# Projecting the values of all heads at once, tokens on the partitions, with attention as one chain over the head pairs

## The chip, the cores and the metric

The kernel runs on one core of one Trainium2 chip. The metric is the device time of one execution in microseconds. Five engines each work through their own list of instructions: TensorE (PE, matrix products; PEld is its weight load), VectorE (DVE), ScalarE (ACT), GpSimd (POOL) and SyncE (SP). The order of each list is fixed when the kernel is built; semaphores hold an instruction until what it needs is there. SBUF is the on-chip memory with 128 partitions, PSUM the eight banks of 128 x 2 KB into which PE writes.

## The reference

One layer of a bidirectional encoder on 512 tokens with 2048 features, in float32. One input projection feeds two mixers that see the same normalised input: a Conformer convolution (1024 channels) and a two-dimensional neighbourhood attention (16 heads of 64) on a grid of 8 rows by 64 columns. The mixers' outputs are normalised each for itself and share one output projection; a gated feed-forward network follows.

```
xn   = rms_norm(x, attn_norm_g)
u_val, u_gate, q, k, v = split(xn @ w_in, [1024, 2048, 3072, 4096])
h      = depthwise_conv31(u_val * sigmoid(u_gate)) + bias
y_conv = silu(layer_norm(h))
y_na   = attention(q, k, v):  a token (r, c) sees all 8 rows and the 16 columns
         clip(c - 8, 0, 48) ... + 15;  softmax(q.k / 8 + rpb[head, dr, dc]) . v
x = x + concat(rms_norm(y_conv, conv_out_g), rms_norm(y_na, na_out_g)) @ w_out
gate, val = split(depthwise_conv3(rms_norm(x, ffn_norm_g) @ w_up))
x = x + (silu(gate) * val) @ w_down
out = rms_norm(x, final_norm_g)
```

## The kernel before

**Products.** Activations lie transposed: 16 tiles of 128 features x 512 tokens. Each float32 operand is split into a high and a low part in the format fp32r, and a product is three matmuls: high by high, high by low, low by high (`mm3`, L121 to L126). In the projections the weights are stationary and the activations move, so the result of `project` comes out with features on the partitions and tokens along the row.

**Weight units.** A unit is 512 KB of weights (128 x 1024): one transfer by SP into a buffer `raw` (ring of NR = 7), a copy to fp32r by ACT (`whi`, L113) and the remainder by DVE (`wlo`, L114), each into a ring of NW = 4. A unit feeds 24 matmuls of 128x512, eight blocks of features by three. `plan` lists the units in the order of use and `weights()` asks for each one AHEAD = 3 units early. One output block of `project` takes two units.

**Order.** `ORDER` says in which sequence output blocks are projected: `a` is one conv projection (gate and value, four units), `q` one pair of heads (q, k and v, six units). After every unit `tick` lets one step of each of two chains of generators run: `steps` (the first norm's statistics, then attention) and `asteps` (`group_a`: layer norm of the conv channels, from the pair NORM_AT on). After the tick, `late` runs `gated` for a finished conv projection: gate by the norm's scale, sigmoid on ACT, again the scale, the product `ch` (L316 to L320), and a conv of 31 taps on DVE: a start (L327, tensor_scalar) and 30 accumulating steps (L331) into `y`. These steps carry a later priority (`shifted(600)`), and the pairs of `y` tiles come out of the same ring `raw` as the weights.

**Who decides.** A scheduler at build time takes these calls with their priorities, its own estimate of times and the free buffers of each ring, and writes each engine's list. `pin` keeps marked instructions in the order of the program.

**Attention, a pair of heads at a time.** A pair is 128 features, and a block of 16 grid columns with all 8 rows (128 queries) sees a window of 32 columns (256 keys). DVE scales q and k by the norm (L383 into block order, L387 plain) and gathers four windows of v (`vw`, L392). `attend` loads four bias tables, turns v on PE (eight transposes `trv`, L411, and two copies `vt` on ACT, L413), and then runs in steps: scores (L425, 16 matmuls in four banks), softmax (DVE L432 scale and add the table, L434 maximum; ACT L437 exponentials with sums; DVE L438 reciprocal; ACT L440 scaling), two turns of the probabilities (`trp`, L450, with copies `pt`, L455), values (L464, 32 matmuls into the bank "po"), a copy `ao` (L484) and the sum of squares (L166, L167).

**Banks.** "mm" three banks for projections; "sc" two banks shared by scores and by the statistics `st`; "tr" two banks for turns and half of the scores; "po" one bank.

**After the projections.** `out_half(ma)` multiplies the conv half of `w_out` (16 units); its results wait in PSUM for the scale `ra` of the conv group's norm (L535). Then `norm_b`, `out_half(mb)` for attention's half, and the feed-forward network, which take three quarters of the time.

## Time and profile before

| | |
|---|---|
| median of three runs | 2055.87 us (2055.01 to 2056.87) |
| the profiled execution | 2055.28 us |
| its span on the core | 2053.5 us |
| mean granted TensorE clock | 0.997 of full |
| PE busy | 2034.3 us, 99% |
| DVE busy | 1663.1 us, 81% |
| ACT busy | 1061.4 us, 52% |
| first matmul of `out_half(ma)` | at 495.2 us |
| its last | at 597.1 us |

The span runs from the first to the last recorded instruction; the device time has 1.8 us more around it. A row of the timeline gives the start, the duration, the engine, the line and operation, and result<-operands; matmuls overlap in the pipeline, so their pace is the distance of their starts, not their duration. A row of a group gives the count, after the bar the busy time in all and the mean of one in ns, and after the second bar how long the engine was idle before them and what it waited for.

### The profile page before, as it was taken

The page shows a single profiled execution, that of the slowest core. Times are in us where ns is not written, and L with a number is a line of the kernel's source. Part 1 is how long each engine was busy: PE and PEld are TensorE (multiplying, and loading weights), DVE is VectorE, ACT ScalarE, POOL GpSimd, SP SyncE. Part 2 cuts the span into 40 slices and gives each one's busy share as a digit, 9 for nine tenths or more (in the row PEclk, how much of TensorE's full clock was granted, in tenths as well). Part 3 has the DMA queues.
Part 4 walks back from the last instruction along what each step waited for, and adds up shares of the span by engine and source line. Part 5 has one row for each costly group of instructions (what it writes and reads, how often), then busy time and mean ns, then how long its engine had stood idle before and what let it go on. Part 6 is the DMA issues. An engine that isn't in the chain of part 4 may idle for free.

```text
span 2053.5 us, 28580 instructions
## 1 busy us (share of the span) xinstructions
PE 2034.3 (99%) x10816; PEld 1736.5 (85%) x10816; DVE 1663.1 (81%) x2319; ACT 1061.4 (52%) x1726; POOL 156.3 (8%) x186
## 2 busy tenths in 40 slices
PE   9999999999999999999999999999999999999997
PEld 7888888887788998888888888888888888888887
DVE  7996697686577898888888878888788888889876
ACT  6244424457445555555555555555554554555562
POOL 0000000000001001111111111111111111110110
PEclk9999999999999999999999999999999999999998
DMA  7332333236237435555465565555555565554672
GB/s 253 109 107 83 100 97 111 84 103 237 82 113 182 127 116 139 127 148 142 120 151 147 124 144 144 130 137 144 135 133 143 126 147 143 133 139 124 148 211 83
DMA packets 97209, 275.38 MB, mean 134 GB/s; under 512 B 10928, under 2 KB 11696, under 8 KB 97072
## 3 DMA queue, kind: packets, MB, share of 16 engines
q1 hardware_dynamic: 71712, 227.40, 34.9%
q0 software_dynamic: 25216, 46.15, 14.8%
q8 instruction: 85, 1.39, 0.3%
q14 instruction: 52, 0.43, 0.1%
q10 hardware_dynamic: 144, 0.01, 0.0%
HBM read 218.99 MB, written 54.53 MB: 133 GB/s over the span
## 4 chain that ended last, share of the span: by engine, by line
PE 94%; DVE 3%; issue 1%; ACT 1%; DMA 1%; SPq 0%; DVEq 0%; ACTq 0%
PE pu L660 23%; PE pu L665 12%; PE pd L126 8%; PE pd L124 8%; PE pd L125 8%; PE pj L124 7%; PE pj L126 7%; PE pj L125 7%; PE po L124 3%; PE po L126 3%; PE po L125 3%; PE pu L124 1%; PE pu L126 1%; PE pu L125 1%; PE sc L425 1%
## 5 line engine op out<-in xcount | busy, mean ns | idle before, releaser
L114 DVE TENSOR_TENSOR wlo<-raw,whi 128x1024 fp32r<-128x1024 f32 x364 | 444.5, 1222 | 246.0 <-ACT whi L113 223.6
L113 ACT ACTIVATE whi<-raw 128x1024 fp32r<-128x1024 f32 x364 | 384.3, 1058 | 489.0 <-PE pj L125 186.2
L660 PE MATMUL pu<-xc,whi 128*128 128x512 f32 x2240 | 573.5, 392 | 0.2 <-ACT pl L672 0.2
L660 PEld LDWEIGHTS pu<-xc,whi 128*128 128x128 f32 x2240 | 408.6, 189 | 74.0 <-ACT pl L672 0.5
L665 PEld LDWEIGHTS pu<-xc,wlo 128*128 128x128 f32 x2240 | 305.6, 190 | 21.9
L665 PE MATMUL pu<-xc,wlo 128*128 128x256 f32 x2240 | 312.3, 282 | 0.0
L124 PE MATMUL pj<-xh,whi 128*128 128x512 f32 x640 | 251.7, 397 | 0.0
L126 PE MATMUL pd<-hh,wlo 128*128 128x512 f32 x640 | 249.1, 391 | 2.2 <-DVE wlo L114 2.2
L126 PE MATMUL pj<-xh,wlo 128*128 128x512 f32 x640 | 250.0, 391 | 0.0
L124 PE MATMUL pd<-hh,whi 128*128 128x512 f32 x640 | 250.0, 391 | 0.0
L125 PE MATMUL pj<-xl,whi 128*128 128x512 f32 x640 | 249.8, 390 | 0.1
L125 PE MATMUL pd<-hl,whi 128*128 128x512 f32 x640 | 249.1, 389 | 0.0
L779 POOL DMA_DIRECT2D x2d<-pdc x160 | 139.3, 872 | 1167.7 <-ACT pdc L778 1064.9
L672 ACT ACTIVATE pl<-pu 128x256 f32<-128x256 f32 x280 | 105.2, 380 | 173.3 <-PE pu L660 173.3
L331 DVE SCALAR_TENSOR_TENSOR y<-ch,prm,y 128x500 f32<-128x500 f32 (+14 forms) x240 | 173.8, 742 | 4.5
L113 ACT ACTIVATE whi<-ws 128x1024 fp32r<-128x1024 f32 x132 | 139.8, 1059 | 67.9 <-PE pu L660 43.5
L114 DVE TENSOR_TENSOR wlo<-ws,whi 128x1024 fp32r<-128x1024 f32 x132 | 161.2, 1221 | 1.3 <-ACT whi L113 1.2
L126 PEld LDWEIGHTS pd<-hh,wlo 128*128 128x128 f32 x640 | 120.2, 188 | 30.9 <-DVE wlo L114 5.7
L124 PEld LDWEIGHTS pj<-xh,whi 128*128 128x128 f32 x640 | 120.1, 188 | 28.7 <-issue 3.9
L778 ACT ACTIVATE pdc<-pd 128x512 f32<-128x512 f32 x160 | 93.9, 588 | 95.9 <-PE pd L126 95.8
L126 PEld LDWEIGHTS pj<-xh,wlo 128*128 128x128 f32 x640 | 120.1, 188 | 26.2 <-DVE wlo L230 0.8
L125 PEld LDWEIGHTS pj<-xl,whi 128*128 128x128 f32 x640 | 120.2, 188 | 25.7 <-issue 1.1
(178 smaller groups left out, 2767.9 us busy)
## 6 DMA issues: line engine op xcount, KB each, us to landing
raw<-in_w_up SPq DMA_DIRECT2D x176, 512.0 KB, 3.6
raw<-in_w_down SPq DMA_DIRECT2D x88, 512.0 KB, 3.6
x2d<-pdc POOLq DMA_DIRECT2D x160, 256.0 KB, 4.6
raw<-in_w_in SPq DMA_DIRECT2D x76, 512.0 KB, 3.7
raw<-in_w_out SPq DMA_DIRECT2D x32, 512.0 KB, 3.8
x<-in_xT SPq DMA_DIRECT2D x32, 256.0 KB, 5.3
tab<-in_tab SPq DMA_DIRECT2D x32, 256.0 KB, 5.1
x2d<-x SPq DMA_DIRECT2D x16, 256.0 KB, 2.2
```

Source lines behind the costliest of these rows:

```text
L113: i = nc.scalar.activation(hi[:, :n], raw[:, :n], AF.Copy)
L114: j = nc.vector.tensor_sub(lo[:, :n], raw[:, :n], hi[:, :n].bitcast(F32))
L124: nc.tensor.matmul(ps, hi[:, a], mh, start=start, stop=False)
L125: nc.tensor.matmul(ps, hi[:, a], ml, start=False, stop=False)
L126: return nc.tensor.matmul(ps, lo[:, a], mh, start=False, stop=stop)
L331: nc.vector.scalar_tensor_tensor(y[:, a:b], h[:, a + j - PAD:b + j - PAD], prm[:, o + j:o + j + 1], y[:, a:b], op0=ALU.mult, op1=ALU.add)
L425: m = nc.tensor.matmul(banks[b // 2 * 2 + j][:, b % 2, :], q[hp, b * P:(b + 1) * P], grid(k, KC0[b], KW)[hp], start=True, stop=True)
L660: return nc.tensor.matmul(ps, w[0][:, k * P:(k + 1) * P], comb[c][k], start=k == 0, stop=k == U - 1)
L665: nc.tensor.matmul(ps[:, H:], w[1][:, k * P:(k + 1) * P], comb[c][k][:, :H], start=False, stop=False)
L672: nc.scalar.activation(to, ps, AF.Copy)
L778: nc.scalar.activation(t, ps, AF.Copy)
L779: nc.gpsimd.dma_start(xd[d], t, accum_op=ALU.add)
```

## The change

1. The values of all 16 heads are projected in one go (`project_v`, step `v` of the order). The activations are stationary (128 tokens of `xh` or `xl` at a time), the weights move (512 of the 1024 value features at a time), so v comes out with tokens on the partitions and needs no turning. There are two halves of features, each into four banks: the first into the three "mm" banks and "po", the second into the two "tr" and the two "sc" banks. A unit of the new input `w_v` holds two blocks of features by 512 columns, and feeds 24 matmuls of 128x512 as before; there are 16 units. ACT copies the results out with the norm's scale per token (`rtok`): eight tiles `vg` and six tiles `vx`, which hold the windows that straddle two 128-token slices.
2. The projection input is regrouped on the host: `xG` holds the tokens in groups of eight grid columns with all rows. q is then written plain, k with a permutation, `ch` and `ao` are written back in the plain token order, and the bias tables are laid out to match. The residual still reads `xT`.
3. Attention is one chain over all pairs in place of a generator for each: for pair p the tables; then the values of pair p-1, the scores and the softmax of p in one tick; a tick of nothing; the turn of the second half of the blocks; the turn of the first. The softmax works in place in the table's tile. There are no `trv`, `vt` and `vw`.
4. The order of projections is `aaaav aq aq aq aq qqqq` (written without gaps), with four units for a `q`, and `group_a` starts at pair 4 in place of 5.

The counts: matmuls 128x512 of the projections stay 1920 (1536 `pj` and 384 `pv`); 64 transposes go from PE, 32 products from DVE; on ACT 16 copies and 4 table loads go and 20 copies come. SP issues 500 transfers in both.

```
-ORDER = "aaqaqaqaaqaqaqqq"
-NORM_AT = 5
+ORDER = "aaaav" + "aq" * 4 + "qqqq"
+NORM_AT = 4
+NG = GW // 8
...
+        if by_token is not None:
+            by_token.append(y)
...
-        last = pin(nc.sync.dma_start(x1[k], xT[k]))
+        last = pin(nc.sync.dma_start(x1[k], xG[k]))
...
+        if step == "v":
+            for half in range(2):
+                for u in range(KD // 2):
+                    plan.append(lambda half=half, u=u: unit(w_v[half, u], U * P))
+            continue
         i = next(a_ if step == "a" else q_)
-        for n in ((NC_ + i, i) if step == "a" else (2 * NC_ + j * NP_ + i for j in range(3))):
+        for n in ((NC_ + i, i) if step == "a" else (2 * NC_ + j * NP_ + i for j in range(2))):
...
+    vg, vx = [], []
+
+    def project_v():
+
+        for half in range(2):
+            if half:
+                sc = psa.tile([P, 2, S], F32, tag="sc", name="pv")
+                banks = [psa.tile([P, S], F32, tag="tr", name="pv", bufs=2) for _ in range(2)] + [sc[:, 0], sc[:, 1]]
+            else:
+                banks = [psm.tile([P, S], F32, tag="mm", name="pv") for _ in range(3)]
+                banks.append(psa.tile([P, S], F32, tag="po", name="pv"))
+            for u in range(KD // 2):
+                wh, wl = weights()[:2]
+                for k in range(2):
+                    kk, f = 2 * u + k, slice(k * S, (k + 1) * S)
+                    for t, ps in enumerate(banks):
+                        xh, xl = (x[:, t * P:(t + 1) * P] for x in xs[kk])
+                        nc.tensor.matmul(ps, xh, wh[:, f], start=kk == 0, stop=False)
+                        nc.tensor.matmul(ps, xl, wh[:, f], start=False, stop=False)
+                        m = nc.tensor.matmul(ps, xh, wl[:, f], start=False, stop=kk == KD - 1)
+                tick(m)
+                while late and rstd:
+                    late.pop(0)()
+            y = rtok[0]
+            vg.append([t2("vg") for _ in banks])
+            vx.append([t2("vx") for _ in banks[1:]])
+            for t, ps in enumerate(banks):
+                nc.scalar.activation(vg[half][t], ps, AF.Copy, scale=y[:, t:t + 1])
+                for x, rows in ((t - 1, slice(0, DH)), (t, slice(DH, P))):
+                    if 0 <= x < len(vx[half]):
+                        nc.scalar.activation(vx[half][x][rows], ps[rows], AF.Copy, scale=y[rows, t:t + 1])
...
-        nc.vector.tensor_mul(h, pv, g)
+        by = "p (g r c) -> p r g c"
+        nc.vector.tensor_mul(h.rearrange("p (r g c) -> p r g c", r=WH, g=NG), pv.rearrange(by, r=WH, g=NG),
+                             g.rearrange(by, r=WH, g=NG))
...
+    def attention():
+
+        before = None
+        for p in range(NP_):
+            while len(qk) <= p:
+                yield
+            ts = tables(p)
+            yield
+            if before:
+                values(*before)
+            banks = scores(p, not before)
+            softmax(banks, ts)
+            yield
+            yield
+            pts = {}
+            pts[2], pts[3] = turn(ts, 2)
+            yield
+            pts[0], pts[1] = turn(ts, 0)
+            before = p, pts
+        yield
+        values(*before)
+        yield
...
+        if step == "v":
+            project_v()
+            continue
         p += 1
-        steps.append(attend(p, *qkv(p)))
+        project_qk(p)
+        if p == 0:
+            steps.append(attention())
         if p == NORM_AT:
             asteps.append(group_a())
```

More of the change, by code (lines that the diff above doesn't have):

```diff
@@ L65, in layer @@
 @with_exitstack
-def layer(ctx: ExitStack, tc: tile.TileContext, xT, w_in, w_out, w_up, w_down, par, tab, out):
+def layer(ctx: ExitStack, tc: tile.TileContext, xT, xG, w_in, w_v, w_out, w_up, w_down, par, tab, out):
     nc = tc.nc
@@ L167, in sum_sq, with rsqrt_steps @@
             nc.vector.tensor_add(acc, acc, q)
-    def rsqrt_steps(accs, n, name, to=slice(0, S), keep=True):
+    def rsqrt_steps(accs, n, name, to=slice(0, S), keep=True, by_token=None):
         if not isinstance(accs, tuple):
@@ L268, in layer @@
             plan.append(lambda half=half, d=d: unit(w_out[half, d], U * P))
-    rstd, late = [], []
+    rstd, rtok, late = [], [], []
     def stats1():
@@ L277, in stats1 @@
             yield
-        rstd.append((yield from rsqrt_steps(acc1, D, "rstd1")))
+        rstd.append((yield from rsqrt_steps(acc1, D, "rstd1", by_token=rtok)))
     steps.append(stats1())
@@ L370, in layer, with project_qk @@
     acc_na = t2("accna")
-    def grid(t, c0, w):
-        return t.rearrange("p (r c) -> p r c", c=GW)[:, :, c0:c0 + w]
-    def qkv(p):
+    qk = []
+    def project_qk(p):
         got = []
-        for j, nm in enumerate("qkv"):
+        for j, nm in enumerate("qk"):
             ps = project(2 * NC_ + j * NP_ + p)
+            t = t2(nm)
             if nm == "q":
-                t = t2(nm)
-                by = "p (r b c) -> p r b c"
-                nc.vector.tensor_mul(t.rearrange("p (b r c) -> p r b c", b=NB, r=WH),
-                                     ps.rearrange(by, b=NB, r=WH), rstd[0].rearrange(by, b=NB, r=WH))
-            elif nm == "k":
-                t = t2(nm)
@@ L387, in qkv @@
                 nc.vector.tensor_mul(t, ps, rstd[0])
             else:
-                t = [t2("vw").rearrange("p (b k) -> p b k", b=2) for _ in range(NB // 2)]
-                for b in range(NB):
-                    nc.vector.tensor_mul(t[b // 2][:, b % 2].rearrange("p (r c) -> p r c", c=KW), grid(ps, KC0[b], KW),
-                                         grid(rstd[0], KC0[b], KW))
+                by = "p (i j c) -> p j i c"
+                nc.vector.tensor_mul(t.rearrange("p (j i c) -> p j i c", i=NB, j=2), ps.rearrange(by, i=NB, j=2),
+                                     rstd[0].rearrange(by, i=NB, j=2))
@@ L394, in qkv, with keys, values_of @@
             got.append(t)
-        return got
-    def attend(p, q, k, v):
-        hps = [slice(j * DH, (j + 1) * DH) for j in range(2)]
-        tabs = {}
+        qk.append(got)
+    def keys(k, b):
+        if b in (0, NB - 1):
+            w = k.rearrange("p (j c) -> p j c", j=2)[:, :, b and P:(b and P) + P]
+        else:
+            w = k[:, b * 64:b * 64 + 384].rearrange("p (j c) -> p j c", j=2)[:, :, :P]
+        return w.rearrange("p j (i c) -> p i j c", i=2)
+    def values_of(p, b):
+        g, x = vg[p // 4], vx[p // 4]
+        return {0: (g[0], g[1]), 1: (x[0], x[1]), 2: (x[1], x[2]), 3: (g[2], g[3])}[b]
@@ L402, in attend, with tables @@
+    hps = [slice(j * DH, (j + 1) * DH) for j in range(2)]
+    def tables(p):
+        ts = {}
         for n in (2, 3, 0, 1):
-            tabs[n] = t2("tab").rearrange("p (i k) -> p i k", i=2)
-            i = nc.sync.dma_start(tabs[n], tab[2 * p + n % 2][:, n // 2:n // 2 + 2])
+            ts[n] = t2("tab").rearrange("p (i k) -> p i k", i=2)
+            i = nc.sync.dma_start(ts[n], tab[2 * p + n % 2][:, n // 2:n // 2 + 2])
             if p == 0:
                 pin(i)
-        vt = []
-        for half in range(2):
-            ps = psa.tile([P, 4, P], F32, tag="tr", name="trv", bufs=2)
-            for c in range(4):
-                nc.tensor.transpose(ps[:, c, :], v[half][:, c // 2, c % 2 * P:(c % 2 + 1) * P], ident)
-            t = t2("vt").rearrange("p (c k) -> p c k", c=4)
-            nc.scalar.activation(t, ps, AF.Copy)
-            vt.append(t)
@@ L415, in attend @@
-        po = psa.tile([P, S], F32, tag="po", name="po")
-        def scores():
-            wide = psa.tile([P, 2, 2, 2 * P], F32, tag="sc", name="sc")
-            banks = [wide[:, j] for j in range(2)]
-            banks += [psa.tile([P, 2, 2 * P], F32, tag="tr", name="sc", bufs=2) for _ in range(2)]
-            first = True
-            for b in range(NB):
-                for j, hp in enumerate(hps):
-                    m = nc.tensor.matmul(banks[b // 2 * 2 + j][:, b % 2, :], q[hp, b * P:(b + 1) * P],
-                                         grid(k, KC0[b], KW)[hp], start=True, stop=True)
+        return ts
@@ new lines, in scores @@
+    def scores(p, first):
+        q, k = qk[p]
+        wide = psa.tile([P, 2, 2, 2 * P], F32, tag="sc", name="sc")
+        banks = [wide[:, j] for j in range(2)]
+        banks += [psa.tile([P, 2, 2 * P], F32, tag="tr", name="sc", bufs=2) for _ in range(2)]
+        for b in range(NB):
+            for j, hp in enumerate(hps):
+                m = nc.tensor.matmul(banks[b // 2 * 2 + j][:, b % 2, :], q[hp, b * P:(b + 1) * P],
+                                     keys(k, b)[hp], start=True, stop=True)
+                if not first:
+                    pin(m)
+                first = False
+        return banks
@@ new lines, in softmax @@
+    def softmax(banks, ts):
+        for n in (2, 3, 0, 1):
+            s = ts[n]
+            nc.vector.scalar_tensor_tensor(s, banks[n], DH ** -0.5, s, op0=ALU.mult, op1=ALU.add)
+            nm = sm.tile([P, 2], F32, tag="nm", name="nm")
+            nc.vector.tensor_reduce(nm, s, axis=AX.X, op=ALU.max, negate=True)
+            su = sm.tile([P, 2], F32, tag="su", name="su")
+            for i in range(2):
+                nc.scalar.activation(s[:, i], s[:, i], AF.Exp, bias=nm[:, i:i + 1], accum_out=su[:, i:i + 1])
+            nc.vector.reciprocal(su, su)
+            for i in range(2):
+                nc.scalar.activation(s[:, i], s[:, i], AF.Copy, scale=su[:, i:i + 1])
@@ L427, in scores, with turn @@
+    def turn(ts, b0):
+        pts, first = [], True
+        for j in range(2):
+            s = ts[b0 + j]
+            ps = psa.tile([P, 4, P], F32, tag="tr", name="trp", bufs=2)
+            for i in range(2):
+                for ch in range(2):
+                    m = nc.tensor.transpose(ps[:, 2 * i + ch, :], s[:, i, ch * P:(ch + 1) * P], ident)
                     if not first:
@@ L429, in scores @@
                     first = False
-            for n in (2, 3, 0, 1):
-                s = t2("s").rearrange("p (i k) -> p i k", i=2)
-                nc.vector.scalar_tensor_tensor(s, banks[n], DH ** -0.5, tabs[n], op0=ALU.mult, op1=ALU.add)
-                nm = sm.tile([P, 2], F32, tag="nm", name="nm")
-                nc.vector.tensor_reduce(nm, s, axis=AX.X, op=ALU.max, negate=True)
-                su = sm.tile([P, 2], F32, tag="su", name="su")
-                for i in range(2):
-                    nc.scalar.activation(s[:, i], s[:, i], AF.Exp, bias=nm[:, i:i + 1], accum_out=su[:, i:i + 1])
-                nc.vector.reciprocal(su, su)
-                for i in range(2):
-                    nc.scalar.activation(s[:, i], s[:, i], AF.Copy, scale=su[:, i:i + 1])
-                soft[n] = s
@@ L443, in turn @@
-        def turn(b0):
-            first = True
-            for j in range(2):
-                s = soft[b0 + j]
-                ps = psa.tile([P, 4, P], F32, tag="tr", name="trp", bufs=2)
-                for i in range(2):
-                    for ch in range(2):
-                        m = nc.tensor.transpose(ps[:, 2 * i + ch, :], s[:, i, ch * P:(ch + 1) * P], ident)
-                        if not first:
-                            pin(m)
-                        first = False
-                pt = t2("pt").rearrange("p (c k) -> p c k", c=4)
-                nc.scalar.activation(pt, ps, AF.Copy)
-                pts[b0 + j] = pt
@@ L458, in values @@
-        def values():
-            first = True
-            for b in range(NB):
-                for ch in range(2):
-                    for j in (1, 0):
-                        hp = hps[j]
-                        m = nc.tensor.matmul(grid(po, b * BLK, BLK)[hp], vt[b // 2][:, 2 * (b % 2) + ch, hp],
-                                             pts[b // 2 * 2 + j][:, 2 * (b % 2) + ch, :], start=(ch == 0), stop=(ch == 1))
-                        if not first:
-                            pin(m)
-                        first = False
@@ L470, in attend, with values @@
-        soft, pts = {}, {}
-        yield
-        scores()
-        yield
-        yield
-        if p < NORM_AT:
-            yield
-        turn(2)
-        yield
-        turn(0)
-        yield
-        yield
-        values()
+            pt = t2("pt").rearrange("p (c k) -> p c k", c=4)
+            nc.scalar.activation(pt, ps, AF.Copy)
+            pts.append(pt)
+        return pts
+    def values(p, pts):
+        po = psa.tile([P, S], F32, tag="po", name="po")
+        first = True
+        for b in range(NB):
+            for ch, v in enumerate(values_of(p, b)):
+                for j in (1, 0):
+                    f = (p % 4 * 2 + j) * DH
+                    m = nc.tensor.matmul(po[hps[j], b * P:(b + 1) * P], v[:, f:f + DH],
+                                         pts[b // 2 * 2 + j][:, 2 * (b % 2) + ch, :], start=(ch == 0), stop=(ch == 1))
+                    if not first:
+                        pin(m)
+                    first = False
@@ L483, in attend @@
         ao = t2("ao")
-        nc.scalar.activation(ao, po, AF.Copy)
+        nc.scalar.activation(ao.rearrange("p (r g c) -> p r g c", r=WH, g=NG),
+                             po.rearrange("p (g r c) -> p r g c", r=WH, g=NG), AF.Copy)
         aos.append(ao)
         sum_sq(acc_na, ao, p == 0)
+    def attention():
[18 more added lines that the diff above has]
+        values(*before)
@@ L889 @@
     xT = np.ascontiguousarray(a["x"][0].T).reshape(KD, P, S)
-    w_in = np.ascontiguousarray(_units(a["w_in"][0]))
+    xG = np.ascontiguousarray(xT.reshape(KD, P, WH, NG, 8).transpose(0, 1, 3, 2, 4)).reshape(KD, P, S)
+    wi = a["w_in"][0]
+    w_in = np.ascontiguousarray(_units(wi[:, :2 * CONV + 2 * NA]))
+    w_v = np.ascontiguousarray(wi[:, 2 * CONV + 2 * NA:].reshape(KD // 2, 2, P, 2, S).transpose(3, 0, 2, 1, 4)
+                               ).reshape(2, KD // 2, P, 2 * S)
     wo = a["w_out"][0]
@@ L911 @@
     rpb = a["rpb"][0]
-    qr, qc = np.divmod(np.arange(P), BLK)
-    kr, kc = np.divmod(np.arange(2 * P), KW)
+    at = np.arange(2 * P)
+    qr, qc = at[:P] % 64 // 8, at[:P] // 64 * 8 + at[:P] % 8
+    kr = at % 64 // 8
     tab = np.full((HEADS, 3, P, 2 * P), NEG, rpb.dtype)
@@ L916 @@
         c = b * BLK + qc[:, None]
+        i, j = at // P, at // 64 % 2
+        kc = (2 * i + (1 - j if kind == 1 else j)) * 8 + at % 8
         k = KC0[b] + kc[None, :]
@@ L921 @@
     tab = np.ascontiguousarray(tab.transpose(0, 2, 1, 3))
-    arrays = {"xT": xT, "w_in": w_in, "w_out": w_out, "w_up": w_up, "w_down": w_down,
+    arrays = {"xT": xT, "xG": xG, "w_in": w_in, "w_v": w_v, "w_out": w_out, "w_up": w_up, "w_down": w_down,
               "par": np.ascontiguousarray(par), "tab": tab}
```

## The prediction

> **What bounds the kernel now.** I read the page first: the busy shares, the chain that ended last, then what TensorE (PE) waited for, because only a stream that never waits can be lengthened by its own work alone.

> ```profile
> span 2053.5 us, 28580 instructions
> PE 2034.3 (99%) x10816; PEld 1736.5 (85%) x10816; DVE 1663.1 (81%) x2319; ACT 1061.4 (52%) x1726; POOL 156.3 (8%) x186
> PE 94%; DVE 3%; issue 1%; ACT 1%; DMA 1%; SPq 0%; DVEq 0%; ACTq 0%
> ```
> ```profile
> PE pd L126 <- DVE wlo L114: 2.2, 8, 0.3
> PE po L124 <- DVE oa L535: 1.9, 1, 1.9
> PE rb L200 <- DVE dg L195: 1.9, 1, 1.9
> PE st L181 <- DVE acc L167: 0.9, 1, 0.9
> ```

> PE is busy for 99% of the span and carries 94% of the chain. In the second view (waited for: total, times, longest) no wait of PE passes 1.9 us; `rb` and `st` are those of the last norm, at the kernel's end. So PE's instructions count at their full pace, work of VectorE (DVE), ScalarE (ACT) and the DMA queues counts only where PE must wait for it, and the kernel has almost no waiting left to give back. The pace is read from PE's timeline (start, duration):

> ```profile
> 84.70 0.39 PE L126 MATMUL pj<-xh,wlo 128*128 128x512 f32 x1
> ...
> 90.82 0.40 PE L126 MATMUL pj<-xh,wlo 128*128 128x512 f32 x1
> 91.05 1.04 PE L411 MATMUL trv<-ident,vw 128*128 128x128 f32 x8
> ...
> 94.69 0.39 PE L124 MATMUL pj<-xh,whi 128*128 128x512 f32 x1
> ...
> 97.19 0.39 PE L126 MATMUL pj<-xh,wlo 128*128 128x512 f32 x1
> 97.50 2.00 PE L425 MATMUL sc<-k,q 64*128 64x256 f32 x16
> 99.43 0.50 PE L124 MATMUL pj<-xh,whi 128*128 128x512 f32 x1
> ```

> From 84.70 to 90.82 lie 27 starts: 0.2267 us each, 5.44 us for a weight unit of 24.

> **1. Turning v on PE goes: -7.4 us.** From the start at 90.82 to the one at 94.69 are 3.87 us; 13 intervals of 0.2267 would be 2.95. One insertion of eight transposes therefore costs 0.92 us, and there are eight: -7.4 (bounds -6.5, eight times 1.04 less one interval, and -8.3, eight times 1.04). Nothing hides PE's work, so all of it is gained. The 16 `vt` copies on ACT and the 32 `vw` products on DVE go too; both lay beside PE: nothing.

> **2. Values and scores in one tick: -1.0.** Between 97.19 and 99.43, 2.24 us, sixteen score matmuls displaced the stream: 0.24 more than their own 2.00. Putting the previous pair's values right ahead of the scores saves one such switch for each of seven pairs: 0 to -2, middle taken.

> **3. The v matmuls themselves: 0.** 384 of 128x512 take the place of 384 of 128x512 (pair by pair before, 48 for each of eight). New are the operands' roles and the rotation over four PSUM banks. The start of the kernel rotates over two:

> ```profile
> 22.38 0.61 PE L124 MATMUL pj<-xh,whi 128*128 128x512 f32 x2
> ...
> 23.74 0.61 PE L124 MATMUL pj<-xh,whi 128*128 128x512 f32 x2
> ```

> Six matmuls on two banks in 1.36 us, 0.227 each: the rotation is free; no row has weights as the moving operand, bounds -1 to +2 (384 times a hundredth of the interval, doubled). Strided products cost nothing visible either: q, strided before, and k, plain, take the same, so exchanging their roles moves nothing; `ch` is taken at its own duration:

> ```profile
> L383 DVE TENSOR_TENSOR q<-pj,rstd 128x512 f32<-128x512 f32 x8 | 5.5, 686 | 0.3 <-PE pj L126 0.3
> L387 DVE TENSOR_TENSOR k<-pj,rstd 128x512 f32<-128x512 f32 x8 | 5.5, 684 | 0.0
> L320 DVE TENSOR_TENSOR ch<-pj,gate 128x512 f32<-128x512 f32 x8 | 5.5, 690 | 0.2
> ```

> The 20 scaled copies `vg`/`vx` stand on ACT between `whi` of units asked for three units (16.3 us) ahead: hidden while that lead lasts. SP issues as many transfers as before, sixteen of `w_v` for sixteen of `w_in`; its queue keeps its order.

> **4. A new wait at the first v unit: +9.3.** This decides the forecast. DVE works in the order fixed at build time. In the changed kernel it holds no `wlo` between the last unit of the fourth conv projection (a3) and the first of v:

> ```
> wlo (a3, last unit) | 14 conv | gate | 2 conv | gate | 13 conv | ch (waits for a3's last matmul)
>   | 4 conv | conv start (tensor_scalar) | 7 conv | wlo (v, first unit) | wlo (v, second) | ...
> PE: a3's last matmul | whi.xh, whi.xl, whi.xh, whi.xl | first matmul with v's wlo | ...
> ```

> Before, three more `wlo` (of v and of the next conv projection) stood inside this stretch. Up to that last `wlo` of a3 the two kernels hold the same number of instructions of the same kinds on DVE, so the clock time is read from before:

> ```profile
> 75.10 0.68 DVE L387 TENSOR_TENSOR k<-pj,rstd 128x512 f32<-128x512 f32 x1
> 75.79 1.23 DVE L114 TENSOR_TENSOR wlo<-raw,whi 128x1024 fp32r<-128x1024 f32 x1
> 76.94 4.70 DVE L331 SCALAR_TENSOR_TENSOR y<-ch,prm,y 128x511 f32<-128x511 f32 x7
> 81.54 1.22 DVE L114 TENSOR_TENSOR wlo<-raw,whi 128x1024 fp32r<-128x1024 f32 x1
> ```
> ```profile
> L318 DVE TENSOR_TENSOR gate<-gate,rstd 128x512 f32<-128x512 f32 x8 | 5.5, 690 | 17.7 <-ACT gate L317 17.7
> L327 DVE TENSOR_SCALAR y<-ch,prm 128x512 f32<-128x512 f32 x8 | 4.3, 544 | 0.2
> ```

> Seven conv steps run from 76.94 to 81.54: 0.657 each. From 76.94 on: 40 conv steps 26.3, three products (two gate, one ch) at 0.69 less the overlap of 0.08 that the conv rows show 1.8, the conv start 0.5, the `wlo` itself 1.2: the first v `wlo` is there at 106.7. PE ends a3's first half at 91.05 (there `trv` starts before; now nothing does), a3 at 96.5 after 24 intervals, and four matmuls that need no `wlo` bring it to 97.4. Wait: 9.3. (`ch` itself isn't held up: DVE reaches it at 97.2.) Bounds 8.7 and 9.9, from a conv step 0.015 shorter or longer, an allowance of mine for reading its pace from one group of seven. The waits of later v units are nil, for their `wlo` follow 1.2 to 1.9 us apart against 5.44 a unit. Queued behind the late `wlo` on DVE are only those, and conv steps that nobody waits for until group A's statistics.

> **5. The clock after it: +2.0.** In windows of the trace (PE, PEld, DVE, ACT, POOL busy, then the granted clock, DMA share, GB/s):

> ```profile
> 517.00:518.00 1.00, 0.00 (x0) 0.00 (x0) 1.00 (x2) 0.97 (x3) 0.00 (x0) 1.00 0.00 0
> ```
> ```profile
> 2042.00:2043.00 1.00, 0.39 (x2) 0.40 (x3) 0.46 (x2) 0.00 (x0) 0.00 (x0) 1.00 0.00 0
> 2043.00:2044.00 1.00, 1.00 (x4) 0.43 (x2) 0.60 (x2) 0.00 (x0) 0.00 (x0) 0.53 0.00 0
> 2044.00:2046.00 2.00, 0.21 (x1) 0.00 (x0) 2.00 (x6) 0.38 (x1) 1.28 (x2) 0.50 0.39 131
> ```
> ```profile
> 1.64 2.48 PE L239 MATMUL idle<-warm 128*128 128x512 f32 x8 [1.64 <-DVE warm L236]
> 4.05 1.77 PE L243 MATMUL idle<-warm 64*128 64x512 f32 x12
> 5.75 0.50 PE L124 MATMUL pj<-xh,whi 128*128 128x512 f32 x1
> ```

> One wait of 1.9 us left the clock at 1.00; the thin end of the kernel dropped it to half. Nine idle microseconds should drop it. The price of coming back is bounded by the start: the eight warm-up matmuls (2,464 columns by the code) took 2.41 us where the later pace gives 1.09, the next twelve (2,048 columns, two half arrays side by side) 1.70 for 0.91. Lost 2.1 in all; bounds 0 and 2.1, and 2.0 is taken since the gap is long.
> [...]

> **6. Group A's statistics and the end of attention: +1.8 and +3.5.** All conv projections now come sooner relative to attention, and four pure q steps end the order, so the last pairs' softmax meets group A's statistics. Rows that price it:

> ```profile
> L484 ACT ACTIVATE ao<-po 128x512 f32<-128x512 f32 x8 | 4.8, 598 | 7.2 <-PE po L464 7.2
> L166 ACT ACTIVATE sq<-ao 128x512 f32<-128x512 f32 x7 | 4.4, 632 | 0.2
> L167 DVE TENSOR_TENSOR accna<-accna,sq 128x512 f32<-128x512 f32 x7 | 4.8, 685 | 1.6 <-ACT sq L166 1.6
> L432 DVE SCALAR_TENSOR_TENSOR s<-sc,tab 128x512 f32<-128x512 f32 x32 | 20.5, 683 | 0.9 <-PE sc L425 0.9
> L437 ACT ACTIVATE s<-s,nm 128x256 f32<-128x256 f32 x64 | 31.7, 496 | 14.7 <-DVE nm L434 14.6
> L440 ACT ACTIVATE s<-s,su 128x256 f32<-128x256 f32 x64 | 28.5, 496 | 4.2 <-DVE su L438 4.0
> L455 ACT ACTIVATE pt<-trp 128x512 f32<-128x512 f32 x32 | 17.4, 589 | 23.3 <-PE trp L450 23.3
> L187 ACT ACT_TABLE_LOAD x3 | 3.8, 1283 | 0.0
> ```

> A matmul of the statistics follows pair 5's scores at once on PE and reuses their "sc" banks, which the second softmax product frees: `ao` 0.60, square 0.63, sum 0.69, two products 1.37 make 3.28 after the values; the scores cover 2.0 of it, and four handovers between engines add about 0.5: +1.8 (bounds 0, if the conv sums make the statistics late on their own account, and 2.2).
> In the first half of the output projection three waits come where there is one of 1.9. (i) `ra`'s statistics: their square root stands on ACT behind eight exponentials, eight scalings, two `pt` and a table load, 9.7 in all with overlaps of 0.1, plus some 1.3 on DVE; PE has 31 matmuls and two groups of transposes, 8.9: 2. (ii) Pair 6's values need two `pt` that stand behind a `whi` (1.06) waiting for the matmul just ahead: 1.06 plus two at 0.5: 2.1. (iii) Pair 7's turn comes one unit (5.44) after scores whose softmax needs 6.4 (a sum, four products, a maximum, three exponentials, a scaling): 1.0. With 0.3 of small ones 5.4, less 1.9: +3.5. These are tallies through several queues; bounds -1.9 (all hidden) to +5.

> **Sum.** -7.4 - 1.0 + 0 + 9.3 + 2.0 + 1.8 + 3.5 = +8.2. On the profiled execution (2055.28; its span 2053.5 and 1.8 around it) this gives 2063.5; the median of the runs, 2055.87, lies 0.59 above it, so 2064.

> **The rivals.** *The v weights are ready in time* (other side). If the first v `wlo` is there by 97.4, terms 4 and 5 vanish: and with the end of attention hidden too, 2055.87 - 8.4 + 1.8 = 2049.3; with its waits, 2052.8. For it: before, with the same conv load, DVE kept its lead; against it: the fixed order above, where 9.3 us would have to come from conv steps of half the measured 0.657. It decides when that wait, with the end hidden, falls under 2.5. Chance 0.08.
> *The wait comes, clock and end stay unharmed:* -8.4 + 9.3 + 1.8 = +2.7, 2058.6. For it: ACT is busy 52% of the span, so the queues of term 6 may drain sooner; against it: the drop in the last windows. Chance 0.17.
> *The end's waits join and drop the clock again:* 2.0, 2.1 and 1.0 lie within few units; one or two more returns at 2.0 give 2066 to 2068. For it: waits of 0.9 (`st`) and 1.9 (`rb`) with narrow matmuls between did it in the tail; against it: between these PE works whole units. Chance 0.13.

> **How the numbers follow.** Forecast 0.62, the rest as above. 0.2% is 4.1 us, about what a measurement of this kernel can tell from no change: slower begins at 2060.0, faster ends at 2051.8. Forecast and third rival are slower, 0.75; the second, and the first where the end's waits stay, lie within: 0.19; faster 0.06. The range reaches to the second rival's lower side (term 4 at 8.7, term 6 at 1 less) and the third's upper, 2057 to 2068.

> **What would show it.** Rows of `trv`, `vw`, `vt` are gone and PE's stream between insertions keeps 0.227 (terms 1 to 3). PE has one wait of about 9 us for DVE's `wlo`, beginning near 97 us, with the granted clock about 0.5 in the windows behind it (4, 5). PE waits of 1 to 2 us for `pt`, `dg` and the "sc" banks stand between 440 and 570 us (6). The forecast is wrong if that first wait is absent, if v matmuls with moving weights leave the pace of 0.227, or if the later waits pass 9 us together.

## The result, and the profile after

The changed kernel takes 2064.1 us (median of six runs, 2063.79 to 2064.95) against 2056.1 of the kernel before on the same chip: 1.0039 times, 95% interval 1.0029 to 1.0050. The forecast was 2064. Its profiled execution took 2063.96, with a span of 2062.2.

The page's first lines, the counterparts of those of before:

```profile
span 2062.2 us, 28425 instructions
PE 2030.1 (98%) x10752; PEld 1735.0 (84%) x10752; DVE 1650.6 (80%) x2287; ACT 1060.2 (51%) x1726; POOL 156.3 (8%) x186
issue 52%; PE 38%; POOL 6%; DVE 2%; DMA 1%; ACT 0%; POOLq 0%; DVEq 0%; ACTq 0%
```

PE is busy 4.2 us less (2034.3 before) in a span 8.7 us longer, so it waits 12.9 us more; matmuls that run at half clock count as busy (2.00 us of the 2.00 from 108.00 on, below, at a granted clock of 0.50). The third line, the chain that ended last, runs through "issue" in this execution and not through PE; with a PE busy for 98% that says little of the bound. The waits of PE do (waited for: total, times, longest):

```profile
PE pv L321 <- DVE wlo L115: 9.2, 1, 9.2
PE st L182 <- DVE tab L471: 2.6, 2, 1.4
PE pd L127 <- DVE wlo L115: 2.2, 8, 0.3
PE po L504 <- ACT pt L493: 1.9, 1, 1.9
PE rb L203 <- DVE dg L198: 1.9, 1, 1.9
...
PE st L182 <- DVE acc L168: 0.9, 1, 0.9
...
PE trp L488 <- ACT tab L479: 0.6, 1, 0.6
```

The first line is the forecast's fourth term: one wait of 9.2 us for the first `wlo` of the v projection. The second, fourth and last are those of the statistics and of the last pairs (term 6); the wait for `oa` of before (1.9) is gone. `rb` and `st <- acc` are the kernel's end, as before. The place in PE's and in DVE's timeline:

```profile
97.25 0.39 PE L320 MATMUL pv<-whi,xl 128*128 128x512 f32 x1
106.80 1.22 PE L321 MATMUL pv<-wlo,xh 128*128 128x512 f32 x2 [9.17 <-DVE wlo L115]
107.82 0.63 PE L319 MATMUL pv<-whi,xh 128*128 128x512 f32 x1
...
110.38 0.50 PE L319 MATMUL pv<-whi,xh 128*128 128x512 f32 x1
110.72 0.40 PE L320 MATMUL pv<-whi,xl 128*128 128x512 f32 x1
110.95 0.40 PE L321 MATMUL pv<-wlo,xh 128*128 128x512 f32 x1
```
```profile
97.32 0.68 DVE L361 TENSOR_TENSOR ch<-pj,gate 128x512 f32<-128x512 f32 x1
97.92 2.68 DVE L373 SCALAR_TENSOR_TENSOR y<-ch,prm,y 128x498 f32<-128x498 f32 x4
100.52 0.54 DVE L369 TENSOR_SCALAR y<-ch,prm 128x512 f32<-128x512 f32 x1
100.98 4.63 DVE L373 SCALAR_TENSOR_TENSOR y<-ch,prm,y 128x503 f32<-128x503 f32 x7
105.53 2.35 DVE L115 TENSOR_TENSOR wlo<-raw,whi 128x1024 fp32r<-128x1024 f32 x2
```

DVE does not idle: it works through four conv steps, the start of a `y` at 100.52 and seven more steps before it comes to the two `wlo`. Behind the wait the matmuls start 0.43 us apart until 110.38, and from 110.72 on 0.23. From 106.80 to 110.72 lie nine intervals, 2.04 at the full pace; they took 3.92, so 1.88 is lost. The windows (granted clock after the five engines) show why:

```profile
98.00:100.00 2.00, 0.00 (x0) 0.00 (x0) 2.00 (x5) 0.00 (x0) 0.00 (x0) 1.00 0.00 0
100.00:102.00 2.00, 0.00 (x0) 0.00 (x0) 2.00 (x4) 0.00 (x0) 0.00 (x0) 0.59 0.00 0
...
108.00:110.00 2.00, 2.00 (x7) 1.52 (x6) 2.00 (x3) 0.00 (x0) 0.00 (x0) 0.50 0.88 297
110.00:112.00 2.00, 2.00 (x9) 1.64 (x8) 2.00 (x3) 0.00 (x0) 0.00 (x0) 0.85 0.90 338
```

By the shares of 0.59 and 0.85 the clock falls to half at 100.4, 2.7 us into the idle stretch, and comes back at 110.6, 3.8 us after the work does. The same happened, unforeseen, behind the short wait of group A's statistics (PE's timeline):

```profile
457.30 1.02 PE L182 MATMUL st<-ones,acc 128*128 128x1 f32 x8 [1.45 <-DVE tab L471]
458.18 0.48 PE L125 MATMUL pj<-xh,whi 128*128 128x512 f32 x1
458.50 0.40 PE L126 MATMUL pj<-xl,whi 128*128 128x512 f32 x1
458.73 0.59 PE L127 MATMUL pj<-xh,wlo 128*128 128x512 f32 x1
459.12 0.63 PE L125 MATMUL pj<-xh,whi 128*128 128x512 f32 x1
...
462.11 0.43 PE L126 MATMUL pj<-xl,whi 128*128 128x512 f32 x1
462.38 0.39 PE L127 MATMUL pj<-xh,wlo 128*128 128x512 f32 x1
```

A wait of 1.45 us and eight matmuls one column wide, then ten intervals that take 3.88 us from 458.50 to 462.38 in place of 2.27: 1.6 lost. Behind the wait of 1.17 before the `ra` statistics (to 504.47) it happened again: the granted clock is 0.50 from 506.6 to 510.0. The twelve intervals of wide matmuls from 505.36 on, with one group of transposes among them, take 4.88 us; in a further execution of the same kernel, whose clock stayed full there, the same twelve take 3.30. So 1.6 is lost here too.

### The profile page after: what moved, and what is told of

Its sections match the earlier page's. It is cut to its first block, busy times and chain, and to the rows that moved or that the text cites. A ratio compares the mean times of both kernels' runs of the same rounds, so it can differ in the third digit from the quotient of the medians.

```text
span 2062.2 us, 28425 instructions
## 1 busy us (share of the span) xinstructions
PE 2030.1 (98%) x10752; PEld 1735.0 (84%) x10752; DVE 1650.6 (80%) x2287; ACT 1060.2 (51%) x1726; POOL 156.3 (8%) x186
## 4 chain that ended last, share of the span: by engine, by line
issue 52%; PE 38%; POOL 6%; DVE 2%; DMA 1%; ACT 0%; POOLq 0%; DVEq 0%; ACTq 0%
POOL x2d L833 6%; PE pj L125 5%; PE pj L127 5%; PE pj L126 5%; PE po L125 2%; PE po L126 2%; PE po L127 2%; PE pu L714 2%; PE pv L321 1%; PE pd L125 1%; PE pd L127 1%; PE pd L126 1%; PE pv L319 1%; PE pv L320 1%; DVE y L373 1%
## 5 line engine op out<-in xcount | busy, mean ns | idle before, releaser
L114 ACT ACTIVATE whi<-raw 128x1024 fp32r<-128x1024 f32 x364 | 384.3, 1058 | 486.9 <-PE pd L126 127.8
L126 PE MATMUL pd<-hl,whi 128*128 128x512 f32 x640 | 249.1, 389 | 0.0
L125 PE MATMUL pj<-xh,whi 128*128 128x512 f32 x512 | 200.9, 397 | 0.0
L127 PE MATMUL pj<-xh,wlo 128*128 128x512 f32 x512 | 200.7, 392 | 0.0
L126 PE MATMUL pj<-xl,whi 128*128 128x512 f32 x512 | 200.4, 391 | 0.0
L114 ACT ACTIVATE whi<-ws 128x1024 fp32r<-128x1024 f32 x132 | 139.8, 1059 | 68.0 <-PE pu L714 43.5
L373 DVE SCALAR_TENSOR_TENSOR y<-ch,prm,y 128x498 f32<-128x498 f32 (+14 forms) x240 | 170.3, 740 | 3.4
L126 PEld LDWEIGHTS pd<-hl,whi 128*128 128x128 f32 x640 | 120.2, 188 | 25.6
L125 PEld LDWEIGHTS pd<-hh,whi 128*128 128x128 f32 x640 | 120.5, 188 | 21.9
L125 PEld LDWEIGHTS pj<-xh,whi 128*128 128x128 f32 x512 | 96.8, 189 | 21.9 <-issue 2.1
```

What stands on the lines that cost most here:

```text
L114: i = nc.scalar.activation(hi[:, :n], raw[:, :n], AF.Copy)
L125: nc.tensor.matmul(ps, hi[:, a], mh, start=start, stop=False)
L126: nc.tensor.matmul(ps, hi[:, a], ml, start=False, stop=False)
L127: return nc.tensor.matmul(ps, lo[:, a], mh, start=False, stop=stop)
L373: nc.vector.scalar_tensor_tensor(y[:, a:b], h[:, a + j - PAD:b + j - PAD], prm[:, o + j:o + j + 1], y[:, a:b], op0=ALU.mult, op1=ALU.add)
```

## The experiments

Theory: the wait of 9.2 us is made by the order of instructions, and this order by the ring `raw`, from which weights and `y` both take buffers. The `y` of the third conv projection comes ahead of the first v unit in the ring's sequence, but its first writer carries the later priority of the conv; until that start is placed, no later unit gets its place on ACT and DVE. Rivals: DVE is simply behind with its conv steps; the v projection itself (operand roles, layout of its weights) makes the wait.

### v behind the second conv projection

```
-ORDER = "aaaav" + "aq" * 4 + "qqqq"
+ORDER = "aavaa" + "aq" * 4 + "qqqq"
```

> The changed kernel with the order of projections aavaa aq aq aq aq qqqq: the v projection stands behind the second conv projection in place of the fourth; nothing else differs. Theory (the shared ring fixes the order): the first v unit is asked for before the conv result y of the third conv projection takes its buffer of the ring, so its low part comes early on VectorE; the wait of 9.2 and the half clock behind it (1.9) fall away, 2064.1 - 11.1 = 2053.0, and the waits of the statistics and of the last pairs stay (1.5, 1.2, 1.9, 0.6). Rival (v matmuls with moving weights, or the switch of operands, cost the time): the v stage is as long as before, 2062 to 2065.

Measured: 2053.1 (2049.7 to 2059.1), ratio to the kernel before 0.9991, interval 0.9979 to 1.0003: no longer slower. No wait for `wlo` is left in the v stage. Its waits beside that:

```profile
PE st L182 <- DVE tab L471: 2.9, 2, 1.5
...
PE po L504 <- ACT pt L493: 1.9, 1, 1.9
```

The 384 v matmuls take 87.04 us from start to start, 0.2267 each: the pace of the stationary weights. The v projection is not the cause. Behind the second of the two waits of the statistics (1.49, to 491.65) the clock is halved here as well, though this kernel has no long wait:

```profile
494.00:496.00 2.00, 2.00 (x7) 1.51 (x7) 0.75 (x2) 2.00 (x8) 0.00 (x0) 0.50 1.06 386
```

### Four conv projections in a row, in the kernel before

```
-ORDER = "aaqaqaqaaqaqaqqq"
-NORM_AT = 5
+ORDER = "aaaa" + "qa" * 4 + "qqqq"
+NORM_AT = 4
```

> The kernel before, with the order aaaa qa qa qa qa qqqq and group A from pair 4 on; v is projected pair by pair as ever. Theory (four conv projections in a row make the wait, not the v projection): TensorE waits 9 to 10 us for the low part of the first q unit near 97 us, with the clock at half behind it; 2056.1 + 9.6 + 1.9 = 2067.6, less up to 1.9 where the wait for oa goes: 2065.5 to 2068. Rival (the v projection or its weights' layout makes the wait): no wait over 2 us there, 2054 to 2058.

Measured: 2066.0, ratio 1.0047 (1.0032 to 1.0062). The wait is there without any v projection (waits of PE, then its timeline):

```profile
PE pj L126 <- DVE wlo L114: 9.6, 1, 9.6
```
```profile
106.72 0.80 PE L126 MATMUL pj<-xh,wlo 128*128 128x512 f32 x1 [9.62 <-DVE wlo L114]
107.31 0.63 PE L124 MATMUL pj<-xh,whi 128*128 128x512 f32 x1
107.74 0.63 PE L125 MATMUL pj<-xl,whi 128*128 128x512 f32 x1
```

It is the order `aaaa` that makes it, with the half clock behind it (2.9 us of it, 1.4 lost by the same count).

### The conv results in a ring of their own

```
-NR = 7
+NR = 3
...
-                ypair.append(t4([P, 2, S], "y"))
+                ypair.append(wpool.tile([P, 2, S], F32, tag="y", name="y", bufs=4))
```

> The changed kernel in its own order aaaav, with the conv results y in a ring of their own (four buffers) and three left for the weights raw, the same memory in all. Theory (sharing the ring ties the v weights to the late start of the third conv's y): the wait of 9.2 goes though VectorE has the same conv work, 2052 to 2054. Rival (VectorE is simply behind by its conv steps): a wait of 5 to 9 us for a low part stays, perhaps one or two v units later, 2060 to 2064.

Measured: 2070.0, a miss in time. The wait in question went nevertheless. Waits of PE:

```profile
PE pd L125 <- ACT whi L114: 3.9, 2, 2.3
PE pd L127 <- DVE wlo L115: 3.8, 2, 2.3
```

There is none for `pv`; `pd` are products of the feed-forward network. There three buffers for weights are too few: ACT waits 59.3 us in all for transfers of `w_down`, and in the changed kernel it shows no such wait. DVE's timeline shows the ring's part:

```profile
82.69 1.22 DVE L115 TENSOR_TENSOR wlo<-raw,whi 128x1024 fp32r<-128x1024 f32 x1
...
106.60 0.54 DVE L369 TENSOR_SCALAR y<-ch,prm 128x512 f32<-128x512 f32 x1
```

The first `wlo` of v comes at 82.69, and the start of the third conv's `y` keeps its later priority and comes at 106.60, even later than the 100.52 above. With the buffers apart the late start no longer holds the weights. But this kernel changes two things at once, so its time says nothing of the gain. A sharper edit followed.

### Only the start of y at once

```
-        with shifted(600):
-            if i % 2 == 0:
-                ypair.append(t4([P, 2, S], "y"))
-            y = ypair[-1][:, i % 2]
-            o = POFF["dww"] + i * CK
-            nc.vector.tensor_scalar(y, h, ...)
+        if i % 2 == 0:
+            ypair.append(t4([P, 2, S], "y"))
+        y = ypair[-1][:, i % 2]
+        o = POFF["dww"] + i * CK
+        nc.vector.tensor_scalar(y, h, ...)
+        with shifted(600):
             for j in range(CK):
```

> The changed kernel in its own order aaaav, where only the first of the 31 conv steps (the tensor_scalar that begins y and takes its buffer of the shared ring) loses its later priority; the other 30 keep it. Theory (the v weights are ordered behind the late start of the third conv's y in the shared ring): the wait of 9.2 for the first v low part and the half clock behind it go, 2053.0, as with the v projection moved, and nothing else changes by more than 0.5. Rival (the ring doesn't matter, VectorE's load of conv steps does; the own ring of four only helped by its other buffers): the wait stays at 5 to 9 us, 2060 to 2064.

Measured: 2052.2, ratio to the kernel before 0.9978 (0.9967 to 0.9989). DVE's timeline:

```profile
75.35 1.23 DVE L115 TENSOR_TENSOR wlo<-raw,whi 128x1024 fp32r<-128x1024 f32 x1
76.50 0.54 DVE L367 TENSOR_SCALAR y<-ch,prm 128x512 f32<-128x512 f32 x1
76.95 4.04 DVE L372 SCALAR_TENSOR_TENSOR y<-ch,prm,y 128x510 f32<-128x510 f32 x6
80.90 1.22 DVE L115 TENSOR_TENSOR wlo<-raw,whi 128x1024 fp32r<-128x1024 f32 x1
```

One instruction of 0.54 us has moved from 100.52 to 76.50, and the next `wlo` follows at 80.90 in place of 105.53, with all conv steps still to be done. Same order of projections, same conv work, same buffers: with the own ring, where a late start did no harm, this shows that the late start of `y` in the shared ring was the cause, and a lack of DVE time was not.

### The wait filled with matmuls

```
                 wh, wl = weights()[:2]
+                if half == 0 and u == 0:
+                    fill = psa.tile([P, 2, S], F32, tag="sc", name="fill")
+                    for j in range(40):
+                        pin(nc.tensor.matmul(fill[:, j % 2], xs[0][0][:, :P], xs[0][0], start=True, stop=True))
```

> The changed kernel with 40 more matmuls of 128x512 (9.1 us, their result is not used) ahead of the first v matmul, into the idle sc banks. Theory (the idle stretch halves the clock, and this costs 1.9 us): the wait shrinks to 0 to 0.5, the granted clock stays at 1.00 in the windows behind, and the kernel is 1.9 us faster though it does more: 2062.2. Rival (the slow matmuls after the wait are the price of the new operand roles or of weights arriving late): they stay at 0.43 us apart, and the time at 2064 to 2065.

Measured: 2061.9, 2.2 less than the changed kernel, with 40 matmuls more. PE's timeline and the clock:

```profile
96.12 9.23 PE L318 MATMUL fill<-xh 128*128 128x512 f32 x40
...
107.40 0.39 PE L323 MATMUL pv<-whi,xh 128*128 128x512 f32 x1
107.63 0.40 PE L324 MATMUL pv<-whi,xl 128*128 128x512 f32 x1
```
```profile
108.00:110.00 2.00, 2.00 (x11) 1.64 (x10) 2.00 (x4) 0.00 (x0) 0.00 (x0) 1.00 0.82 297
```

The matmuls keep their 0.23 and the clock is full, so it was the idle stretch that halved the clock here, and the loss behind it is term 5. The 2.2 is no clean measure of it: the mean granted clock of this profile is 0.997 against 0.994, and half clock in other places may be missing from it too.

### The statistics' wait filled

```
+        if name in ("rln", "ra"):
+            fill = psa.tile([P, S], F32, tag="po", name="fill")
+            for j in range(6):
+                pin(nc.tensor.matmul(fill, xs[0][0][:, :P], xs[0][0], start=True, stop=True))
         for b, acc in enumerate(accs):
```

> The changed kernel with six more matmuls of 128x512 (1.4 us, result unused, into the po bank) ahead of the statistics matmuls of group A's two norms; the first wait of 9.2 stays. Theory (an idle stretch of 1.2 to 1.5 us plus eight matmuls one column wide is enough to halve the clock): both waits fall to about 0.4, the clock stays at 1.00 behind them, and 1.7 + 1.6 come back, less up to 1.2 for statistics later than before: 2061 to 2062.5. Rival (the clock falls for another reason, such as the load of the memory around 506 us): it still falls, 2064 to 2065.

Measured: 2067.2 (2064.0 to 2068.3), the profiled execution 2063.98: a miss. Behind the first statistics the wait and the half clock are gone (the wide matmuls from 458.34 to 460.87 start 0.23 apart). Ahead of the second a wait of 1.5 remains: the second six matmuls got their place at 509.54, behind the statistics at 502.50, so that half of the theory wasn't tested. The twelve added matmuls cost PE 3.0 us. The filling paid back what it took and no more; why the median lies 3 us above the profiled execution isn't settled.

### The changed kernel three times more

> The changed kernel once more, unaltered, for one more profiled execution. Theory (the clock is judged in windows of about 3.4 us that run free of the kernel): the waits stay where they are (9.2 at 97, 1.5 at 456, 1.2 at 503), the half clock after the first is there each time, with 1.4 to 2.4 us lost, but the half clock after the short ones comes in some executions and not in others. Rival (the work around the wait decides): half clock after 456 and 503 in every execution, 1.6 and 1.1 us each.

> As for the first further execution: same waits; by the theory of free windows the half clock after the waits of 1.5 and 1.2 differs between executions, by the rival it is the same in all.

> As for the first further execution: same waits; by the theory of free windows the half clock after the waits of 1.5 and 1.2 differs between executions, by the rival it is the same in all.

Measured, one execution each: 2064.0, 2067.9, 2063.4. The 9.2 us wait stood in all, and counted as above it lost 2.2, 2.6 and 1.8 behind it (1.9 in the first profile). Behind the wait of 1.45 the half clock (granted clock 0.50) came in all four executions. Behind the one before the `ra` statistics it came in two of four, and where it didn't, a wait of 1.3 for the scale's `dg` followed 10 us later. Yet in the kernels with v after two and with y started at once the same wait of 1.45 us (to 445.78 and to 445.54) left the granted clock at 1.00 through 450.

Where the changes of the clock lie decides between theory and rival. In the first profile windows narrowed around a change give its time to 0.01 us. In the other executions the share of a window of 2 us gives it to 0.02, as here in the second further execution, where 0.78 and 0.66 mean 0.88 and 1.36 us at half clock:

```profile
100.00:102.00 2.00, 0.00 (x0) 0.00 (x0) 2.00 (x4) 0.00 (x0) 0.00 (x0) 0.78 0.00 0
...
110.00:112.00 2.00, 2.00 (x7) 1.54 (x6) 2.00 (x4) 0.00 (x0) 0.00 (x0) 0.66 0.97 348
```

| execution | falls to half and rises to full, us |
|---|---|
| changed kernel, first profile | 100.37 and 110.61, 458.77 and 462.18, 506.56 and 509.97, the last fall at 2052.79 |
| changed kernel, first further | 100.92 and 111.16, 459.32 and 462.72 |
| changed kernel, second further | 101.12 and 111.36, 459.52 and 462.92, 507.32 and 510.72 |
| changed kernel, third further | 99.52 and 109.76, 457.92 and 461.36 |
| v after two | 493.76 and 497.16 |

| wait | most in one stretch, us | clock in the next stretch |
|---|---|---|
| first statistics, changed kernel, four executions | 2.33, 2.33, 2.05, 2.33 | half in all |
| first statistics, v after two | 1.62 | full |
| `ra` statistics, changed kernel, four executions | 2.06, 1.87, 1.93, 1.64 | half, full, half, full |
| `ra` statistics, v after two | 2.21 | half |
| plain wait of 1.89 for `pt`, changed kernel, first profile | 1.21 | full |

In these eleven cases the next stretch ran at half clock from 1.93 up, and at full clock up to 1.87. That is what the theory of free windows expected, and the rival's half clock after 503 in every execution did not come. Four of four behind the first wait was then chance: whether a wait of this size halved the clock went with how much of it the lines left in one stretch (2.33 or 2.05, half; 1.62, full). The clock came back on such a line too, so the loss behind the 9.2 us wait varies with the place of the restart: 3.6 to 5.3 us at half clock in these four executions.

### Eight transposes fewer in the kernel before

```
-            ps = psa.tile([P, 4, P], F32, tag="tr", name="trv", bufs=2)
-            for c in range(4):
-                nc.tensor.transpose(ps[:, c, :], v[half][:, c // 2, c % 2 * P:(c % 2 + 1) * P], ident)
...
-            nc.scalar.activation(t, ps, AF.Copy)
+            nc.scalar.activation(t.rearrange(...), v[half].rearrange(...), AF.Copy)
```

> The kernel before without the eight transposes of v for each pair: ScalarE copies the gathered v windows as they are, so the values are computed from v in the wrong arrangement. Theory (each insertion costs TensorE 0.92 us, nothing hides it): 2056.1 - 7.4 = 2048.7, up to 0.9 more where the wait for oa grows. Rival (part of it lies beside the matmuls' pipeline): -3 to -5, 2051 to 2053.

Measured: 2050.3, ratio 0.9968 (0.9954 to 0.9982), 6.5 below the kernel before. The wait for `oa` grew:

```profile
PE po L124 <- DVE oa L534: 2.8, 1, 2.8
```

That is 0.9 more than the 1.9 of before; 6.5 and 0.9 make the 7.4 of term 1. The interval of the ratio, 3.7 to 9.5 us, is too wide to rule out the rival's 5 by itself; the count in the trace of before, below, does.

### Group A earlier, its statistics in another bank

On top of the kernel that starts `y` at once:

```
-NORM_AT = 4
+NORM_AT = 3
-RA_AFTER = 5
+RA_AFTER = 4
...
-        banks = [psa.tile([P, 2, S], F32, tag="sc", name="st")[:, 0]]
+        one = len(accs) == 1 and keep
+        banks = [psa.tile([P, S], F32, tag="po", name="st") if one else psa.tile([P, 2, S], F32, tag="sc", name="st")[:, 0]]
...
             nc.vector.tensor_add(acc, acc, ys[i])
         yield
+        yield
```

> As the kernel with y started at once, and group A one pair earlier (NORM_AT 3, one more step before its first statistics, RA_AFTER 4), with its statistics in the po bank in place of the sc banks. Theory (statistics behind the scores wait for the sc banks, and wait plus narrow matmuls halve the clock each time): the waits of 1.5 and 1.2 with 1.7 and 1.6 of half clock go, and those of 1.9 and 0.6 in the first half of the output projection too, for group A is ready sooner; one wait of 1.5 for a scale comes. 2053.0 - 8.4 + 1.5 = 2046.1, faster than both kernels. Rival (these waits only move): 2051 to 2054.

Measured: 2044.1 (2043.7 to 2046.1), ratio to the kernel before 0.9937 (0.9921 to 0.9953): faster than both. All of PE's waits:

```profile
PE pd L127 <- DVE wlo L115: 2.1, 8, 0.3
PE rb L204 <- DVE dg L199: 1.9, 1, 1.9
PE idle L243 <- DVE warm L240: 1.6, 1, 1.6
PE pu L715 <- ACT pl L727: 1.1, 1, 1.1
PE st L183 <- DVE acc L168: 0.9, 1, 0.9
PE st L183 <- DVE acc L651: 0.9, 1, 0.9
PE pu L125 <- ACT xc L604: 0.7, 1, 0.7
```

Not one is left in the projections, attention or the first half of the output projection; even the expected wait of 1.5 for a scale stayed away, which is most of the 2 us by which it beat its expectation. Several things were changed together here, so their shares aren't told apart.

## Why the prediction was right

| term | forecast | measured |
|---|---|---|
| 1 turning v goes | -7.4 | -7.4 |
| 2 values and scores in one tick | -1.0 | -1.5 |
| 3 the v matmuls | 0 | 0 |
| 4 wait for the first v `wlo` | +9.3 | +9.2 |
| 5 half clock behind it | +2.0 | +1.9 |
| 6 statistics, end of attention: waits | +5.3 | +3.2 |
| half clock behind two of these | in a rival | +3.2 |
| sum | +8.2 | +8.6; profiled executions +8.7, medians +8.0 |

**Terms 1 to 3.** In the trace of before the eight insertions of `trv` lengthen the stream by 7.39 us (from the last wide matmul ahead to the third behind, less the regular intervals: seven of 0.89 and, less its wait for `oa`, one of 1.16), and the run without them agrees. By the same count scores cost 2.15 and values 2.11 by themselves, and 4.04 together in the changed kernel: 0.22 for each of seven pairs. The forecast's 0.24 came close by another way: the 2.24 it was read from still holds one regular interval of 0.23. Rotating banks and moving weights cost nothing here, as the 0.2267 shows.

**Term 4** came out to 0.1 because both sides of it, DVE's list up to the wait and PE's up to the same unit, could be counted in steps whose pace the trace of before has. The forecast read the wait off the instruction order without asking what made that order; the runs supplied the cause, and with it the cure.

**Term 5.** The price bounded from the cold start (0 to 2.1, 2.0 taken) held in the first profile; over four executions it was 1.8 to 2.6, so the upper bound was too low, and a single figure was the wrong form: in these executions it went with where the restart fell between the lines. From the restart to the return the half clock lasted 3.8 us in the first profile, and from 2.9 (four conv projections first) to 5.3 over the runs.

**Term 6** was right in kind and wrong in sizes. The statistics waited 1.45 (1.8 forecast), pair 6's values 1.89 (2.1), pair 7's turn 0.57 (1.0). In the first of these the four handovers were put at 0.5, and no run shows that: in the trace `ao`, its square and the sum each start 0.03 to 0.04 behind what they wait for, and with some 0.15 for four the same tally gives 1.4. Item (i) failed as told: in the first profile `ra`'s statistics did not wait 2 for their scale behind the square root; they waited 1.17 for the "sc" banks, one step earlier. What held the banks was a transfer: DVE's softmax products (500.65) waited 1.10 for the pair's bias tables, which SP issues from 491.25 on. In the four executions this wait is 1.10, 1.21, 1.61 and 0.69, and the statistics wait 0.06 to 0.07 longer each time. The forecast has no term for it.

What the waits fell short, 2.1, the clock took back: the third rival's mechanism, the clock dropping again, came true at the two statistics (1.6 each). Of the end's waits, where the rival had put it, only the one for `ra` did this. So the total owes its fit to luck in part: two misses of 2.1 and 3.2 in opposite directions, of which the second differs from one execution to the next. What the table leaves, 0.1, is less than the change in small waits of the feed-forward network, such as 0.9 for `pl` where 0.2 stood before.

**The rivals.** The first, no wait at all, is what the kernel becomes when v moves or `y` starts at once: 2053.1 and 2052.2, where 2052.8 was worked out for it with the end's waits in place.

## What to carry to other kernels

Where PE never waits, the sum of moved work says less than the order of the lists: walk the list of the engine that feeds PE from the change on, step by step at the paces of the trace, and see when the first operand arrives. A ring of buffers shared by urgent tiles and by tiles with a later priority passes the delay on to everything allocated behind; give the first write of the late tile its normal place, or a ring of its own if the memory allows it. Price an idle stretch of the matmul engine with its return to full clock, as a range (1.8 to 2.6 us behind the 9.2 here), and count a short wait next to narrow matmuls as one that may halve the clock in some executions and not in others (two of four before the `ra` statistics).

## What the runs showed of the hardware that was not expected

In the five executions of the table with the times of the changes (four of the changed kernel, one of the kernel with v after two) all the changes of the granted clock that it lists lie on lines a whole number of 3.413 us apart, and these lines lie differently in each execution of the same kernel: the first fall comes 2.55 to 4.22 us after the start of the same wait. Less than a whole stretch of rest was enough to halve the clock for the next one: 1.93 us or more of waiting and one-column matmuls within one stretch did it in seven cases of seven, 1.87 or less in none of four. So a wait of 1.45 us followed by 0.9 us of one-column matmuls halved the clock in all four executions of the changed kernel, and left it at 1.00 in the profiles with v after two and with y started at once. These figures go by the ends of matmuls as the profile gives them, which are modelled.
